# Activations of 32 tokens by gathered rows, U products of 352 columns, 20 odd chunks and 24 gathers in the gate stage

## The chip, the cores and the metric

The kernel runs on one core of a Trainium2 chip. The metric is the device time of one execution in microseconds (us). The kernel before took 1524.5 us, the median of 3 runs (1523.61 to 1525.55).

## What is computed

One decoder block for 512 tokens of width 1024, all in float32: attention and gated linear attention side by side, then a mixer over 16384 experts (PEER), then a final norm. The change lies in the mixer. Each token picks 128 experts (8 heads with 16 each) by two rounds of top-16 and gets a gate for each; every expert has a row of `u` and a row of `v`.

```python
def peer_ffn(h, wq, subkeys, u, v):
    ...
    expert = jnp.take_along_axis(cand_i, best_pos, axis=-1)
    gates = jax.nn.softmax(best_v, axis=-1).astype(h.dtype)
    ...
    def block(args):
        xb, eb, gb = args
        ub = jnp.take(u, eb, axis=0)
        hid = jax.nn.gelu(jnp.einsum('tkd,td->tk', ub, xb), approximate=False) * gb
        vb = jnp.take(v, eb, axis=0)
        return jnp.einsum('tk,tkd->td', hid, vb)
```

## The kernel before

The 512 tokens are four blocks of 128. Blocks 0 to 2 are the dense ones (`DENSE`, 384 tokens, `TD`): for them PE multiplies with all 16384 experts, in 128 chunks of 128 experts, and the gates, written out as a dense matrix that is zero for experts that were not picked, select. Block 3 (`GB`, the gathered block) gets its rows of `u` and `v` by 128 + 128 gathers, each of 128 rows of 4 KB (one expert for each token), and DVE multiplies and adds them up.

A float32 product is made of three products in the fp32r form (`mm3`, L68 to L71): each operand is split into a high part (a copy by ACT, L64) and a low part (a subtraction by DVE or POOL, L65).

**U part** (`u_part`, L692). For a chunk c, PE makes 8 x 3 = 24 products of a 128x128 piece of `u` by the tokens' activations; the result `ph` has one column for each dense token but the last `TS` = 16 (`TU` = 368 columns). ACT takes the Gelu (L705) into `ge`. The chunks of `AHEAD`, the 64 even ones, are computed ahead, while queries, routing and gates are made; their `ge` goes to DRAM (`gsp`, on ACT's queue) and is read back later. The 64 odd ones are computed in the V stage, each some 8 chunks ahead of its use (`LEAD`), and stay in a ring of `RING` = 6.

**Sparse rows** (`sp_index`, `sp_rows`, `sp_gather`, `sp_dot`, `sp_finish`, L930 to L975). The last 16 dense tokens get their activations otherwise: each gather fetches 128 rows of `u` (16 tokens by 8 of their 128 experts), and DVE makes the dot products with the tokens' own rows, 16 gathers and 16 dots in all, with 2 buffers. The result times the gate replaces the gate of these tokens, so that the dense gate matrix already holds the activation there.

**Gate stage.** For each dense block and each group of 16 tokens, `gate_group` makes one-hot matrices on DVE (`o12`, L895), multiplies them by the gates (`o2`, L911), and PE multiplies the two (`pg`, 24 short products each half group, L918); ACT copies the result (L920), and it is stored as `Gd` in DRAM. There are 24 groups, each with two halves. In this stage the order of DVE and POOL is that of the program (`manual_schedule`); PE, ACT and SP are ordered by the scheduler. A loop over the pieces of work (`woven`, `work`) keeps a running sum of what DVE and PE were given, by written costs (`DVE_ALL`, `PE_ALL`, `UCOST`), and calls the next U chunk whenever PE's share falls behind. The pieces are the groups, the sparse dots between their halves, the routing of the blocks, and at the end of the stage `EARLY` = 8 of the gathered block's 128 dots (`ahead`, `dots_of`), one after each group of the third block. One-hot matrices and gathered rows share a ring of 5 buffers (`gr`, `GR`).

**V stage.** For each of the 128 chunks, `v_part` loads the rows of `v` (two chunks a load), splits them, multiplies the gates by the Gelu values (L1169), splits the product (`Ah` L1173, `Al` L1174, four buffers each), and PE adds 18 products of 512 columns into the six accumulators (`v_matmuls`). After every second chunk comes the next odd U chunk. `gather_to` spreads the remaining gathers over the chunks: `gather_u` (a gather of `u` rows on POOL, a dot on DVE, L1003) and `gather_v` (a gather of `v` rows, added into `gacc`, L1016), with 7 buffers. At the end `finish` scales each block, adds the residual, norms it and stores it; the gathered block is finished after the last gather, then the dense blocks with the last four chunks (`LAST`).

## Time and profile before

| what | before |
|---|---|
| median of 3 runs | 1524.5 us |
| the profiled execution: its time | 1523.26 us |
| the profiled execution: its span | 1521.5 us |
| granted TensorE clock, mean | 0.991 |
| PE busy | 1460.3 us (96%) |
| DVE busy | 1251.6 us (82%) |
| ACT busy | 677.7 us (45%) |
| POOL busy | 482.2 us (32%) |
| moved by DMA | 417.04 MB, mean 274 GB/s |
| PE's share of the chain that ended last | 89% |

The stages follow one another: conditioning, projections and both mixers to about 290 us, queries and top-k to about 420, routing and gates to about 705, the V stage to about 1503, the last norms to the end. Busy times are per engine; matmuls overlap in their rows, so the distance from start to start is their cost.

### The profile page before, as it was taken

How to read it: one execution, taken by the hardware profiler on the slowest of the kernel's cores; microseconds unless marked ns; L12 is line 12 of the kernel's file. 1: busy time of each engine (PE TensorE's matmuls, PEld its weight loads, DVE VectorE, ACT ScalarE, POOL GpSimd, SP SyncE). 2: the span in 40 equal slices, each digit the busy share in tenths (PEclk: the TensorE clock that was granted, in tenths of full speed). 3: DMA queues.
4: the chain of work that ended last, by engine and by line, in shares of the span. 5: the costliest groups of instructions: out<-in, count | busy, mean ns of one | idle time of the engine just before them, and what ended most of it. 6: DMA issues, size and time to landing. Idle time of an engine off the chain costs nothing.

```text
span 1521.5 us, 24401 instructions
## 1 busy us (share of the span) xinstructions
PE 1460.3 (96%) x9387; PEld 1301.7 (86%) x9387; DVE 1251.6 (82%) x2389; ACT 677.7 (45%) x1072; POOL 482.2 (32%) x344
## 2 busy tenths in 40 slices
PE   4999989899999999999999999999999999999995
PEld 3787877888999999999888888888888888888884
DVE  7578657689999999996778878787878878788998
ACT  5545486533344665765333333333333333333332
POOL 1000000145505220222334434453535434454461
PEclk9999999999999999999999999999999999999997
DMA  9253535462446997899999989989999898998894
GB/s 349 99 208 115 175 106 191 152 215 92 140 171 207 305 314 229 257 295 330 411 408 335 334 317 345 357 322 333 343 349 344 326 339 344 357 335 291 312 356 157
DMA packets 158004, 417.04 MB, mean 274 GB/s; under 512 B 11312, under 2 KB 78144, under 8 KB 145472
## 3 DMA queue, kind: packets, MB, share of 16 engines
q1 hardware_dynamic: 107296, 258.18, 47.5%
q0 software_dynamic: 39312, 144.20, 25.9%
q10 hardware_dynamic: 11280, 13.11, 2.5%
q8 instruction: 73, 1.20, 0.3%
q14 instruction: 43, 0.35, 0.1%
HBM read 374.01 MB, written 41.42 MB: 273 GB/s over the span
## 4 chain that ended last, share of the span: by engine, by line
PE 89%; DVE 4%; ACT 3%; DMA 2%; issue 2%; SPq 0%; DVEq 0%; POOL 0%; ACTq 0%; POOLq 0%
PE ph L71 11%; PE ph L69 11%; PE acc L70 11%; PE acc L69 11%; PE ph L70 11%; PE acc L71 11%; PE pg L918 4%; PE pq L69 2%; PE pq L71 2%; PE pq L70 2%; PE pj L71 1%; PE pj L69 1%; PE pj L70 1%; DMA gu<-in_u_dram,ix_u 1%; PE pn L69 1%
## 5 line engine op out<-in xcount | busy, mean ns | idle before, releaser
L993 POOL DMA_INDIRECT gu<-in_u_dram,ix_u x128 | 191.4, 1495 | 314.4 <-DVE gacc L1016 128.8
L1011 POOL DMA_INDIRECT gv<-in_vP_dram,ix_v x128 | 176.8, 1381 | 216.2 <-DVE gu L1003 163.9
L1173 ACT ACTIVATE Ah<-gr 128x384 fp32r<-128x384 f32 x128 | 67.1, 525 | 308.6 <-PE acc L70 305.0
L1016 DVE SCALAR_TENSOR_TENSOR gacc<-gv,hg,gacc 128x1024 f32<-128x1024 f32 x127 | 162.8, 1282 | 0.2
L1003 DVE SCALAR_TENSOR_TENSOR gu<-gu,h2n 128x1024 f32<-128x1024 f32 x128 | 156.0, 1220 | 0.7 <-DMA gu<-in_u_dram,ix_u 0.7
L705 ACT ACTIVATE ge<-ph 128x368 f32<-128x368 f32 x128 | 59.9, 468 | 152.8 <-PE ph L71 152.7
L1174 DVE TENSOR_TENSOR Al<-gr,Ah 128x384 fp32r<-128x384 f32 x128 | 71.0, 556 | 66.4 <-ACT Ah L1173 66.2
L920 ACT ACTIVATE gs<-pg 128x512 f32<-128x512 f32 x96 | 94.1, 1114 | 3.8 <-PE pg L918 2.8
L1066 POOL IOTA iot<- 128x256 bf16 x1 | 1.5, 1540 | 282.2 <-DVE h2Tl L680 282.2
L911 DVE TENSOR_TENSOR o<-o,gp 128x3072 bf16<-128x3072 bf16 x48 | 84.0, 1755 | 0.4 <-PE pg L918 0.4
L959 POOL DMA_INDIRECT spr<-in_u_dram,spix x16 | 40.6, 2535 | 105.6 <-DVE spr L964 61.3
L918 PE MATMUL pg<-o,o 128*128 128x128 bf16 x1152 | 72.7, 218 | 0.5 <-ACT gs L920 0.5
L918 PEld LDWEIGHTS <-o 128*128 128x128 bf16 x1152 | 66.2, 97 | 6.0 <-issue 0.7
L895 DVE TENSOR_TENSOR o<-iot,t 128x2048 bf16<-128x2048 bf16 x48 | 58.4, 1223 | 2.4 <-PE pg L918 2.4
L1169 DVE TENSOR_TENSOR gr<-ge,gr 128x368 f32<-128x368 f32 x64 | 34.5, 540 | 23.3 <-ACT ge L705 23.3
L217 DVE SCALAR_TENSOR_TENSOR macc<-wa,scs,macc 128x1024 f32<-128x1024 f32 x28 | 38.8, 1385 | 5.1 <-DMA wa<-in_w_ada_dram 4.8
L1169 DVE TENSOR_TENSOR gr<-gel,gr 128x368 f32<-128x368 f32 x64 | 31.9, 535 | 2.9 <-DMA gr<-Gd 2.9
L70 PE MATMUL pq<-h2Tl,wq_0h 128*128 128x512 f32 (+1 forms) x80 | 27.9, 349 | 1.2 <-DVE h2Tl L680 1.2
L69 PE MATMUL pq<-h2Th,wq_0h 128*128 128x512 f32 (+1 forms) x80 | 28.0, 352 | 1.0 <-ACT qha L758 1.0
L71 PE MATMUL pq<-h2Th,wq_1l 128*128 128x512 f32 (+1 forms) x80 | 28.1, 352 | 0.0
L70 PE MATMUL pq<-h2Tl,wq_1h 128*128 128x512 f32 (+1 forms) x80 | 28.1, 352 | 0.0
L69 PE MATMUL pq<-h2Th,wq_1h 128*128 128x512 f32 (+1 forms) x80 | 28.0, 350 | 0.0
(2608 smaller groups left out, 5028.3 us busy)
## 6 DMA issues: line engine op xcount, KB each, us to landing
u<-in_uT_dram SPq DMA_DIRECT2D x64, 1024.0 KB, 8.3
v<-in_vP_dram SPq DMA_DIRECT2D x64, 1024.0 KB, 7.5
Gd<-gs SPq DMA_DIRECT2D x23, 1024.0 KB, 8.1
gr<-Gd SPq DMA_DIRECT2D x15, 1536.0 KB, 11.0
wa<-in_w_ada_dram SPq DMA_DIRECT2D x20, 1024.0 KB, 6.3
gsp<-ge ACTq DMA_DIRECT2D x64, 184.0 KB, 4.6
gel<-gsp SPq DMA_DIRECT2D x32, 368.0 KB, 4.8
wi<-in_w_in_dram SPq DMA_DIRECT2D x9, 1024.0 KB, 6.2
```

What stands on the lines that cost most here:

```text
L69: nc.tensor.matmul(acc, lh, rh, start=start, stop=False)
L70: nc.tensor.matmul(acc, lh, rl, start=False, stop=False)
L71: return nc.tensor.matmul(acc, ll, rh, start=False, stop=stop)
L911: nc.vector.tensor_tensor(o2, o12[:, :, 1, None].to_broadcast([P, H, 3, P, 2]), gp3[:, g0:g0 + H, :, None].to_broadcast([P, H, 3, P, 2]), ...
L918: nc.tensor.matmul(pt[:, i, :], o12[:, g, 0, :, r], o2[:, g, m, :, r], start=(m == 0), stop=(m == 2))
L920: nc.scalar.activation(gs[:, :, t0 + 4 * f:t0 + 4 * f + 4].rearrange("p b a -> p a b"), pt, AF.Copy)
L993: nc.gpsimd.indirect_dma_start(out=ur, out_offset=None, in_=a["u"], in_offset=bass.IndirectOffsetOnAxis(ap=ix_u[:, s:s + 1], axis=0))
L1003: nc.vector.scalar_tensor_tensor(ur, ur, 1.0, h2n, op0=OP.mult, op1=OP.mult, accum_out=hid[:, s:s + 1])
L1011: nc.gpsimd.indirect_dma_start(out=vr, out_offset=None, in_=a["vP"], in_offset=bass.IndirectOffsetOnAxis(ap=ix_v[:, s:s + 1], axis=0))
L1016: nc.vector.scalar_tensor_tensor(gacc, vr, hg[:, s:s + 1], gacc, op0=OP.mult, op1=OP.add)
L1173: nc.scalar.activation(grp(Ah), A, AF.Copy)
L1174: nc.vector.tensor_tensor(grp(Al), A, grp(Ah), OP.subtract)
```

## The change

- `TS` goes from 16 to 32 tokens: 32 sparse gathers and dots instead of 16, each of 32 tokens by 4 experts, with 3 buffers and up to three dots a group; the U products have 352 columns instead of 368.
- `AHEAD` gets 20 odd chunks beside the 64 even ones: chunks 4m+1 and 4m+3 for m = 2, 5, ..., 29. The V stage makes 44 U chunks instead of 64. `gsp` is laid out anew so that two odd chunks are read back at once, into a buffer of their own (`gel1`, one; `gel0`, two).
- `EARLY` goes from 8 to 24: two gathers after each group from the middle of the second block on, and their two dots one group later.
- The remaining gathers are spread by a written cost of each chunk instead of evenly, without the lag of 10 between `u` and `v` rows, over the first 118 chunks (`LAST_G`), and the gathered block is finished when chunk 119 is reached.

```diff
--- before.py
+++ after.py
@@ -30,14 +30,15 @@
 GB = 3
 TG = 16
 NGRP = TD // TG
-TS = 16
+TS = 32
 TU = TD - TS
 NGU = TU // TG
 SB = DENSE[-1]
 SR = P // TS
 
 
-AHEAD = tuple(range(0, P, 2))
+ODD_AHEAD = tuple(range(2, 32, 3))
+AHEAD = tuple(c for m in range(P // 4) for c in (4 * m, 4 * m + 2) + ((4 * m + 1, 4 * m + 3) if m in ODD_AHEAD else ()))
 RING = 6
 GR = 5
 TCARGS = dict(schedule_with_timeline_sim=True)
@@ -686,7 +687,7 @@
                     nc.tensor.transpose(pb[:, i * P:(i + 1) * P], h32[:, 4 * half + i, :], ident)
                 nc.scalar.activation(h2n[:, half * 512:(half + 1) * 512], pb, AF.Copy)
 
-    gsp = dr.tile([len(AHEAD), P, TU], F32, name="gsp")
+    gsp = dr.tile([P // 4, 2, 2, P, TU], F32, name="gsp")
     ges, last_gelu = {}, {}
 
     def u_part(c, lo_eng=None, after=None):
@@ -703,8 +704,8 @@
         ge = dnA.tile([P, NGU, TG], F32, tag="ge", bufs=RING, name=f"ge{c}")
         gef = ge.rearrange("p g t -> p (g t)")
         last_gelu["u"] = nc.scalar.activation(gef, ph, AF.Gelu)
-        if c % 2 == 0:
-            nc.scalar.dma_start(gsp[c // 2], gef)
+        if c in AHEAD:
+            nc.scalar.dma_start(gsp[c // 4, c % 2, c // 2 % 2], gef)
         else:
             ges[c] = ge
         return end
@@ -950,20 +951,20 @@
             ps_, cs = slice(r * TS, (r + 1) * TS), slice(r * TS, (r + 1) * TS)
             nc.sync.dma_start(sp["ix"][ps_], e[P - TS:, cs])
             nc.sync.dma_start(sp["g"][ps_], gates[SB][P - TS:, cs])
-        for j in range(2):
+        for j in range(3):
             sp_gather(j)
         yield 0.3, 0
 
     def sp_gather(j):
-        sp[j] = rt.tile([P, D], F32, tag="spr", bufs=2, name=f"spr{j}")
+        sp[j] = rt.tile([P, D], F32, tag="spr", bufs=3, name=f"spr{j}")
         nc.gpsimd.indirect_dma_start(out=sp[j], out_offset=None, in_=a["u"],
                                      in_offset=bass.IndirectOffsetOnAxis(ap=sp["ix"][:, j:j + 1], axis=0))
 
     def sp_dot(j):
         r = sp.pop(j)
         nc.vector.scalar_tensor_tensor(r, r, 1.0, sp["x"], op0=OP.mult, op1=OP.mult, accum_out=sp["hid"][:, j:j + 1])
-        if j + 2 < TS:
-            sp_gather(j + 2)
+        if j + 3 < TS:
+            sp_gather(j + 3)
         yield 1.15, 0
 
     def sp_finish():
@@ -986,7 +987,7 @@
 
     gather_tile.k = -1
 
-    EARLY = 8
+    EARLY = 24
 
     def fetch_u(s):
         ur = gather_tile(f"gu{s}") if s >= EARLY else gp.tile([P, D], F32, tag="gr", bufs=GR, name=f"gu{s}")
@@ -1016,9 +1017,9 @@
             nc.vector.scalar_tensor_tensor(gacc, vr, hg[:, s:s + 1], gacc, op0=OP.mult, op1=OP.add)
 
 
-    VLAG = 10
-    gathers = [(s * 0.88 / NS, gather_u, s) for s in range(NS)]
-    gathers += [((s + VLAG) / (NS + VLAG), gather_v, s) for s in range(NS)]
+    gathers = [(-1, gather_u, s) for s in range(EARLY)]
+    gathers += [((s - EARLY) * 0.88 / (NS - EARLY), gather_u, s) for s in range(EARLY, NS)]
+    gathers += [((s + 0.5) / NS, gather_v, s) for s in range(NS)]
     gathers = [g[1:] for g in sorted(gathers, key=lambda g: g[0])]
 
     def gather_to(upto):
@@ -1093,7 +1094,7 @@
         for q in range(P // TG):
             for i, piece in enumerate(gate_group(DENSE.index(n), n, q)):
                 yield piece
-                if (i == 3 or i == 1 and q % 2 == 0) and rows:
+                if i and rows:
                     yield from sp_dot(rows.pop(0))
             if q in extra:
                 yield from chain(*extra[q])
@@ -1103,14 +1104,19 @@
     first_block = {3: [gate_transposes(1)], 5: [gate_parts(1)], 6: [gate_rest(1)]}
     second_block = {1: [route(GB)], 2: [gathered_index()], 3: [sp_finish()], 5: [gate_transposes(SB)],
                     6: [gate_parts(SB)], 7: [gate_rest(SB)]}
-    third_block = {0: [ahead(0, 1)]}
-    for q in range(1, EARLY):
-        third_block[q] = [dots_of(q - 1, 1), ahead(q, 1)]
-    third_block[EARLY - 1] += [dots_of(EARLY - 1, 1)]
+    third_block = {}
+    places = [(second_block, q) for q in range(3, 8)] + [(third_block, q) for q in range(P // TG)]
+    for i, (block, q) in enumerate(places):
+        pieces = block.setdefault(q, [])
+        if i:
+            pieces.append(dots_of(2 * i - 2, 2))
+        if i < EARLY // 2:
+            pieces.append(ahead(2 * i, 2))
+    assert EARLY == 2 * len(places) - 2
     work = chain(route_heads(), *head, woven(0, rows, first_block), woven(1, rows, second_block),
                  woven(SB, [], third_block))
     NL_U = len(AHEAD) - LAST_U
-    DVE_ALL = 11 + 4 * 7.6 + 3 + 1.15 * TS + 2.82 * 2 * NGRP + 9 + 1.14 * (NL_U - WQ_U)
+    DVE_ALL = 11 + 4 * 7.6 + 3 + 1.15 * TS + 2.82 * 2 * NGRP + 1.15 * EARLY + 1.14 * (NL_U - WQ_U)
     PE_ALL = 1.4 * 2 * NGRP + 3 + UCOST * (NL_U - WQ_U)
     dve_s = ExitStack()
     dve_s.enter_context(tc.manual_schedule(engines={mybir.EngineType.DVE, mybir.EngineType.Pool}))
@@ -1158,11 +1164,11 @@
         if c % CG == 2 and c + CG < P:
             gates_of(c // CG + 1)
         vh, vl = hilo(v_part.raw[:, c % 2], [P, D], f"vc{c}", nc.vector)
-        if c % 2 == 0:
-            if c % 4 == 0:
-                v_part.ge = dnA.tile([P, 2, TU], F32, tag="gel", bufs=2, name=f"gel{c}")
-                nc.sync.dma_start(v_part.ge, gsp[c // 2:c // 2 + 2].rearrange("c p t -> p c t"))
-            ge = v_part.ge[:, c // 2 % 2].rearrange("p (g t) -> p g t", g=NGU)
+        if c in AHEAD:
+            if c % 4 < 2:
+                v_part.ge[c % 2] = dn.tile([P, 2, TU], F32, tag=f"gel{c % 2}", bufs=2 - c % 2, name=f"gel{c}")
+                nc.sync.dma_start(v_part.ge[c % 2], gsp[c // 4, c % 2].rearrange("c p t -> p c t"))
+            ge = v_part.ge[c % 2][:, c // 2 % 2].rearrange("p (g t) -> p g t", g=NGU)
         else:
             ge = ges.pop(c)
         A = v_part.g[:, :, c % CG, :]
@@ -1173,6 +1179,8 @@
         nc.scalar.activation(grp(Ah), A, AF.Copy)
         nc.vector.tensor_tensor(grp(Al), A, grp(Ah), OP.subtract)
         return c, Ah, Al, vh, vl
+
+    v_part.ge = {}
 
     def v_matmuls(parts, blocks=range(len(DENSE)), qs=(0, 1)):
         for c, Ah, Al, vh, vl in parts:
@@ -1203,16 +1211,21 @@
                 nc.vector.scalar_tensor_tensor(y[:, qs], y[:, qs], r, fwb[:, qs], op0=OP.mult, op1=OP.mult)
             nc.sync.dma_start(out[n * P:(n + 1) * P, qs], y[:, qs])
 
-    LEAD = 8
+    LEAD, LAST_G = 8, 118
+    cost = [4.09 + (UCOST if c % 2 == 0 and c + 1 + LEAD < P and c + 1 + LEAD not in AHEAD else 0) for c in range(LAST_G)]
     for c in range(1, 1 + LEAD, 2):
         u_part(c)
     for c in range(P - LAST):
-        if c % 2 == 0 and c + 1 + LEAD < P:
+        if c % 2 == 0 and c + 1 + LEAD < P and c + 1 + LEAD not in AHEAD:
             u_part(c + 1 + LEAD)
         with tc.issue_after(last_gelu["u"].ins) if c < 2 else nullcontext():
             parts = v_part(c)
         v_matmuls([parts])
-        gather_to(len(gathers) * (c + 1) // (P - LAST))
+        gather_to(EARLY + int((len(gathers) - EARLY) * sum(cost[:c + 1]) / sum(cost) + 1e-6))
+        if c == LAST_G + 1:
+            with tc.issue_after(last_gelu["u"].ins), tc.issue_after(last_gelu["hg"].ins):
+                nc.scalar.preload_act_table_set("natural_log_exp_and_others")
+            finish(GB, [gacc[:, 0:512], gacc[:, 512:1024]])
         if c == 16:
             tc.keep_in_program_order(bcast_load(fwb, a["fw"], D))
         if c == P - 16:
@@ -1225,9 +1238,6 @@
                 for i in range(4):
                     nc.tensor.matmul(pb[:, i * P:(i + 1) * P], ones, dg[:, 4 * q + i, :], start=True, stop=True)
                 nc.scalar.activation(h2n[:, q * 512:(q + 1) * 512], pb, AF.Copy)
-    with tc.issue_after(last_gelu["u"].ins), tc.issue_after(last_gelu["hg"].ins):
-        nc.scalar.preload_act_table_set("natural_log_exp_and_others")
-    finish(GB, [gacc[:, 0:512], gacc[:, 512:1024]])
     last = [v_part(c) for c in range(P - LAST, P)]
     xl = dn.tile([P, 2, D], F32, tag="vraw", bufs=2, name="xl")
     for i in range(len(DENSE)):
```

DVE in the first block of the gate stage, some half groups in (`o` from `iot` is a one-hot, `o` from `gp` its product with the gates, `spr` a sparse dot, `uc..l` the low part of a U chunk). Before:

```order
L964 SCALAR_TENSOR_TENSOR spr_4902,sphid<-spr_4902,xs 128x1024
L895 TENSOR_TENSOR o_012_5273<-iot,t_5034 128x2048
L65 TENSOR_TENSOR uc52l<-u_5275,uc52h 128x1024
L911 TENSOR_TENSOR o_010_5309<-o_08_5204,gp_5043 128x3072
L895 TENSOR_TENSOR o_016_5339<-iot,t_5034 128x2048
L911 TENSOR_TENSOR o_018_5341<-o_012_5273,gp_5043 128x3072
L964 SCALAR_TENSOR_TENSOR spr_5202,sphid<-spr_5202,xs 128x1024
L65 TENSOR_TENSOR uc54l<-u_5275,uc54h 128x1024
L895 TENSOR_TENSOR o_020_5408<-iot,t_5034 128x2048
L911 TENSOR_TENSOR o_020_5410<-o_016_5339,gp_5043 128x3072
L964 SCALAR_TENSOR_TENSOR spr_5269,sphid<-spr_5269,xs 128x1024
```

and now:

```order
L965 SCALAR_TENSOR_TENSOR spr_5228,sphid<-spr_5228,xs 128x1024
L896 TENSOR_TENSOR o_016_5405<-iot,t_5062 128x2048
L66 TENSOR_TENSOR uc46l<-u_5338,uc46h 128x1024
L965 SCALAR_TENSOR_TENSOR spr_5267,sphid<-spr_5267,xs 128x1024
L912 TENSOR_TENSOR o_018_5442<-o_012_5336,gp_5071 128x3072
L965 SCALAR_TENSOR_TENSOR spr_5332,sphid<-spr_5332,xs 128x1024
L66 TENSOR_TENSOR uc45l<-u_5475,uc45h 128x1024
L896 TENSOR_TENSOR o_020_5511<-iot,t_5062 128x2048
L912 TENSOR_TENSOR o_020_5513<-o_016_5405,gp_5071 128x3072
L965 SCALAR_TENSOR_TENSOR spr_5403,sphid<-spr_5403,xs 128x1024
L66 TENSOR_TENSOR uc47l<-u_5475,uc47h 128x1024
```

Of eleven rows three were sparse dots and two U chunks; now four are sparse dots and three U chunks, two of them odd (45, 47). The order of one-hot and product is kept, with more between them.

DVE in the V stage, from chunk 12 on (`vc..l` low part of the rows of `v`, `Al` low part of the gated activations, `gu` a dot of a gathered row, `gacc` an addition of one). Before:

```order
L65 TENSOR_TENSOR vc12l<-v_8936,vc12h 128x1024
L65 TENSOR_TENSOR vc13l<-v_8936,vc13h 128x1024
L65 TENSOR_TENSOR uc23l<-u_8903,uc23h 128x1024
L1169 TENSOR_TENSOR gr_8833<-ge_8934,gr_8833 128x23x16
L1016 SCALAR_TENSOR_TENSOR gacc<-gv_9105,hg,gacc 128x1024
L1003 SCALAR_TENSOR_TENSOR gu_9172,hid<-gu_9172,h2n 128x1024
L1174 TENSOR_TENSOR Al_9151<-gr_8833,Ah_9150 128x384
L65 TENSOR_TENSOR vc14l<-v_9037,vc14h 128x1024
L65 TENSOR_TENSOR vc15l<-v_9037,vc15h 128x1024
L1174 TENSOR_TENSOR Al_9185<-gr_8833,Ah_9184 128x384
L1016 SCALAR_TENSOR_TENSOR gacc<-gv_9175,hg,gacc 128x1024
L65 TENSOR_TENSOR uc25l<-u_9108,uc25h 128x1024
```

and now:

```order
L1008 TENSOR_TENSOR hg<-hg,gg_g 128x8
L1180 TENSOR_TENSOR Al_9718<-gr_9132,Ah_9717 128x384
L66 TENSOR_TENSOR vc12l<-v_9610,vc12h 128x1024
L1017 SCALAR_TENSOR_TENSOR gacc<-gv_9506,hg,gacc 128x1024
L66 TENSOR_TENSOR vc13l<-v_9610,vc13h 128x1024
L1004 SCALAR_TENSOR_TENSOR gu_9571,hid<-gu_9571,h2n 128x1024
L1017 SCALAR_TENSOR_TENSOR gacc<-gv_9574,hg,gacc 128x1024
L1180 TENSOR_TENSOR Al_9785<-gr_9542,Ah_9784 128x384
L1004 SCALAR_TENSOR_TENSOR gu_9577,hid<-gu_9577,h2n 128x1024
L66 TENSOR_TENSOR vc14l<-v_9677,vc14h 128x1024
L66 TENSOR_TENSOR vc15l<-v_9677,vc15h 128x1024
L66 TENSOR_TENSOR uc25l<-u_9742,uc25h 128x1024
```

Before, a U chunk's low part stands behind every pair of chunks of `v` (23, 25); now 23 is gone from this place, since it was made ahead, and more dots and additions of gathered rows stand between the pairs.

DVE at the end (`y` from `gacc` is the gathered block's scaling, `y` from `acc` a dense block's). Before:

```order
L65 TENSOR_TENSOR vc126l<-v_14636,vc126h 128x1024
L1016 SCALAR_TENSOR_TENSOR gacc<-gv_14546,hg,gacc 128x1024
L65 TENSOR_TENSOR vc127l<-v_14636,vc127h 128x1024
L1016 SCALAR_TENSOR_TENSOR gacc<-gv_14549,hg,gacc 128x1024
L1016 SCALAR_TENSOR_TENSOR gacc<-gv_14579,hg,gacc 128x1024
L1016 SCALAR_TENSOR_TENSOR gacc<-gv_14582,hg,gacc 128x1024
L1016 SCALAR_TENSOR_TENSOR gacc<-gv_14585,hg,gacc 128x1024
L1192 TENSOR_TENSOR y_14589<-gacc,h2n 128x512 x2
L1192 TENSOR_TENSOR y_14681<-acc_8177,h2n 128x512
L1192 TENSOR_TENSOR y_14681<-acc_8178,h2n 128x512
L1192 TENSOR_TENSOR y_14730<-acc_8179,h2n 128x512
L1192 TENSOR_TENSOR y_14730<-acc_8180,h2n 128x512
```

and now:

```order
L1017 SCALAR_TENSOR_TENSOR gacc<-gv_14457,hg,gacc 128x1024
L1017 SCALAR_TENSOR_TENSOR gacc<-gv_14460,hg,gacc 128x1024
L1180 TENSOR_TENSOR Al_14729<-gr_14287,Ah_14728 128x384
L1200 TENSOR_TENSOR y_14551<-gacc,h2n 128x512 x2
L1201 TENSOR_TENSOR y_14551<-y_14551,xf_14552 128x512
L66 TENSOR_TENSOR vc126l<-v_14712,vc126h 128x1024
L1201 TENSOR_TENSOR y_14551<-y_14551,xf_14552 128x512
L66 TENSOR_TENSOR vc127l<-v_14712,vc127h 128x1024
L1203 TENSOR_TENSOR ssf_14554<-ssf_14554 128x1
L81 TENSOR_SCALAR rf3m<-ssf_14554 128x1
L84 TENSOR_TENSOR rf3t<-rf3y 128x1
L85 TENSOR_TENSOR rf3t<-rf3t,rf3m 128x1
```

Four additions into `gacc` and the gathered block's scaling stood behind the last low part (`vc127l`), with the dense blocks' work right behind; now the additions end ahead of `vc126l`, and that block's output is on its way before a dense block's begins.

## The prediction

> **What bounds the kernel now.** I read the stretches first: busy time of every engine over one stretch each. Columns: stretch, its length, PE, weight load, DVE, ACT and POOL busy with instruction counts, granted clock, DMA share, GB/s.
>
> ```profile
> 405.00:440.00 35.00, 35.00 (x212) 35.00 (x211) 32.54 (x174) 16.14 (x21) 10.28 (x12) 1.00 0.51 179
> 440.00:480.00 40.00, 40.00 (x246) 39.85 (x245) 37.46 (x56) 16.01 (x27) 16.65 (x2) 1.00 0.55 192
> 480.00:510.00 30.00, 30.00 (x261) 29.29 (x260) 28.10 (x27) 16.88 (x22) 8.40 (x5) 1.00 0.78 255
> 510.00:540.00 30.00, 30.00 (x290) 29.15 (x287) 30.00 (x29) 20.01 (x28) 6.92 (x4) 1.00 1.00 315
> 540.00:600.00 60.00, 60.00 (x502) 58.86 (x500) 57.32 (x64) 34.73 (x44) 8.60 (x5) 1.00 0.87 286
> 600.00:660.00 60.00, 59.22 (x604) 57.32 (x603) 55.30 (x47) 43.47 (x54) 11.78 (x3) 1.00 0.81 250
> 660.00:705.00 45.00, 45.00 (x438) 43.87 (x437) 40.83 (x38) 29.65 (x36) 8.58 (x5) 1.00 0.99 315
> 705.00:740.00 35.00, 32.04 (x185) 30.67 (x182) 17.98 (x25) 13.49 (x22) 9.93 (x10) 0.96 0.96 362
> 740.00:800.00 60.00, 60.00 (x296) 52.87 (x295) 49.78 (x68) 21.82 (x32) 24.75 (x18) 1.00 1.02 405
> 800.00:1100.00 300.00, 300.00 (x1472) 263.93 (x1471) 245.27 (x321) 108.43 (x153) 133.23 (x94) 1.00 0.91 337
> 1100.00:1400.00 300.00, 300.00 (x1479) 264.57 (x1478) 243.33 (x318) 108.98 (x154) 130.01 (x93) 1.00 0.92 340
> ```
>
> PE is busy without a hole from 405 to 600 and from 740 to 1400, with some 4 us missing between. In the gate stage (about 420 to 705) DVE is nearly as full, 281.5 of 300 us from 405 to 705; in the V stage it has 18% left. A busy PE need not be at its peak, so I checked the pace in the order of time (start, length, instruction).
>
> ```profile
> 409.22 0.33 PE L69 MATMUL ph<-h2Th,uc12h 128*128 128x368 f32 x1
> 413.22 0.33 PE L69 MATMUL ph<-h2Th,uc14h 128*128 128x368 f32 x1
> ...
> 1498.14 0.39 PE L69 MATMUL acc<-vc127h,Ah 128*128 128x512 f32 x1
> ...
> 1502.22 0.39 PE L69 MATMUL acc<-vc127h,Ah 128*128 128x512 f32 x1
> ```
>
> The first two are the starts of neighbouring U chunks of 24 products: 4.00 us, 166.7 ns each, back to back. Between the other two stand 18 products of 512 columns: 4.08 us, 226.7 ns. From the two widths a column costs 0.417 ns and each product 13 ns beside. So PE streams at one column rate all the time, and only less matmul work, or its few holes, can shorten the run. The waits name the holes (engine, line, cause: us, times, longest).
>
> ```profile
> PE acc L69 <- ACT Ah L1173: 1.9, 1, 1.9
> ...
> PE acc L69 <- ACT vc118h L64: 1.3, 1, 1.3
> ...
> PE ph L71 <- DVE uc124l L65: 1.0, 1, 1.0
> ```
>
> Nothing longer stands after 290 us until the last product.
>
> **Narrower U products.** All 128 chunks keep 24 products and go from 368 to 352 columns: 16 columns by 0.417 ns is 6.67 ns each, 0.16 us a chunk (4.00 to 3.84), 128 x 0.16 = **20.5 us** of PE work. All of it lies in stretches without holes, so I count all of it, as long as nobody else becomes late. Below zero this cannot go: no product is added.
>
> **Twenty odd chunks go ahead.** PE work is only moved: 20 x 3.84 = 76.8 us leave the V stage and enter the gate stage. With them go 20 subtractions on DVE, 20 stores on ACT's queue, and their read-back in the V stage.
>
> **Sixteen more sparse rows, sixteen more early gathers.** This is DVE work in the gate stage, 32 dots. Groups by line, and rows in the order of time:
>
> ```profile
> L1003 DVE SCALAR_TENSOR_TENSOR gu<-gu,h2n 128x1024 f32<-128x1024 f32 x128 | 156.0, 1220 | 0.7 <-DMA gu<-in_u_dram,ix_u 0.7
> L911 DVE TENSOR_TENSOR o<-o,gp 128x3072 bf16<-128x3072 bf16 x48 | 84.0, 1755 | 0.4 <-PE pg L918 0.4
> L895 DVE TENSOR_TENSOR o<-iot,t 128x2048 bf16<-128x2048 bf16 x48 | 58.4, 1223 | 2.4 <-PE pg L918 2.4
> ...
> L964 DVE SCALAR_TENSOR_TENSOR spr<-spr,xs 128x1024 f32<-128x1024 f32 x16 | 19.5, 1222 | 4.6 <-DMA spr<-in_u_dram,spix 4.6
> ```
>
> ```profile
> 706.75 1.22 DVE L65 TENSOR_TENSOR uc126l<-u,uc126h 128x1024 fp32r<-128x1024 f32 x1
> 707.89 1.22 DVE L65 TENSOR_TENSOR uc1l<-u,uc1h 128x1024 fp32r<-128x1024 f32 x1
> ```
>
> A row of 1.22 us is followed by the next start after 1.14 us, so I take 0.08 us off each length. DVE gains 32 x 1.14 + 20 x 1.14 = 59 us in the gate stage, PE gains 76.8 and loses about 70 chunks x 0.16 = 11, net 66. Whether PE stays the longer one is read per token group of 16. The chain gives the gate products:
>
> ```profile
> 497.64 2.77 PE pg L918 x48
> ```
>
> In the first block the changed order puts 20 U chunks and 24 sparse dots into 8 groups. DVE: two one-hots and two products 2 x (1.14 + 1.67) = 5.62, three dots 3.42, 2.5 subtractions 2.85, together 11.9 us; PE: 2.77 + 2.5 x 3.84 = 12.4. In the last block, with 16 U chunks and two early dots a group: DVE 5.62 + 2.28 + 2.28 = 10.2, PE 2.77 + 2 x 3.84 = 10.5. So PE stays the longer one, by 3 to 4%, about 10 us over 24 groups, which is what DVE may lose in new waits before PE pays. The waits of DVE that are there already:
>
> ```profile
> DVE spr L964 <- DMA spr<-in_u_dram,spix: 4.6, 2, 2.7
> DVE hg L1007 <- ACT hg L1006: 3.3, 1, 3.3
> ...
> DVE o L895 <- PE pg L918: 2.4, 4, 0.8
> ```
>
> A sparse row is asked for when the dot three before it is done, one group (12.4 us) earlier; less the dot itself, 11.2 us remain. Issue to landing is 8.4 us in the middle (transfer table):
>
> ```profile
> gu<-in_u_dram,ix_u POOLq DMA_INDIRECT x128, 8.2
> ...
> spr<-in_u_dram,spix POOLq DMA_INDIRECT x16, 8.4
> ```
>
> Behind a late dot stand the next one-hot, the next U subtraction and with it PE. I expect several short waits, mostly inside the 10 us, and charge PE 2 us (bounds 0 and 20). The early gathers wait a group too and hold 2 of the 5 buffers of the one-hots; three one-hots still fit, so I charge nothing, with up to 0.8 us for each of 13 groups (the L895 row) as the other end. The 20 stores on ACT's queue take 0.33 us of issue each,
>
> ```profile
> 698.24 0.33 ACTq L707 DMA_DIRECT2D gsp<-ge  x1
> ```
>
> 7 us in a stage where ACT is under 75% busy in every stretch above: nothing, and if ACT had no room, at most those 7 us.
>
> **The V stage.** Per V chunk DVE pays now 245.27 / 50 = 4.91 us of 6.0 (300 us hold 50 chunks). Its gathers are counted by the transfer table of 800 to 1400, which holds 100 chunks:
>
> ```profile
> gu<-in_u_dram,ix_u POOLq DMA_INDIRECT x95, 8.1
> gv<-in_vP_dram,ix_v POOLq DMA_INDIRECT x91, 7.9
> ```
>
> From 1.86 a chunk they rise to 232 / 118 = 1.97, and U chunks fall from 0.5 to 40 / 118 = 0.34: 4.91 - 0.16 x 1.14 + 0.11 x 1.2 = 4.86 us in 4.08 + 0.34 x 3.84 = 5.38 us, 90% instead of 82%. In runs of four to six V chunks with no U chunk between them it is higher still; four buffers of weights level that out. DVE's largest wait there is for ACT, whose buffers PE holds:
>
> ```profile
> DVE Al L1174 <- ACT Ah L1173: 65.6, 59, 3.6
> ```
>
> So DVE runs ahead of PE, and this slack goes first. I charge 2 us (bounds 0 and 15). Where the stages meet, one U chunk fewer covers the way of the last gates through DRAM:
>
> ```profile
> 702.53 2.93 PE L918 MATMUL pg<-o,o 128*128 128x128 bf16 x48
> ```
>
> ```profile
> 723.61 0.54 DVE L1169 TENSOR_TENSOR gr<-gel,gr 128x368 f32<-128x368 f32 x1 [2.93 <-DMA gr<-Gd]
> ```
>
> The gates were back 18 us after the last gate product; 6 x 3.84 = 23 us of U products stand there then, where 28 stood, so the cover holds by 5 us, and without it the rest of the way would be PE's.
>
> **The end.** The sequence block's gathers end with chunk 117 and its output is finished by chunk 119, not behind the last gather.
>
> ```profile
> 1502.67 0.39 PE L71 MATMUL acc<-vc127h,Al 128*128 128x512 f32 x1
> ...
> 1491.53 5.25 DVE L1016 SCALAR_TENSOR_TENSOR gacc<-gv,hg,gacc 128x1024 f32<-128x1024 f32 x4
> ...
> 1504.10 1.28 DVE L1192 TENSOR_TENSOR y<-acc,h2n 128x512 f32<-128x512 f32 x2
> ...
> 1512.74 3.43 DVE L1203 SCALAR_TENSOR_TENSOR y<-y,rf2y,fwb 128x512 f32<-128x512 f32 x2
> ```
>
> From the last product (1503.1) to the last scaling 9.7 us pass, because DVE still has the gathered block's tail between. Without that block it is a product, an addition and a square (0.64 each), one other block's scaling (1.4) and small steps (2): about 5 us. I take **5 us** off (bounds 2 and 6).
>
> **Sum**, against the profiled execution (span 1521.5, its time 1523.3): 1523.3 - 20.5 - 5 + 2 + 2 = 1501.8. The median of the runs shown lies 1.2 us above that execution: **1503 us**.
>
> **Rivals.**
> *Transfers bind the V stage.* Mean 338 GB/s at a share of 0.915 there; per V chunk 6.0 us x 338 = 2.03 MB. The change trades U loads (0.16 x 0.52 = 0.08 MB less) for denser gathers (0.11 x 0.52 = 0.06 more) and read-backs (0.03 more), so 2.03 MB must pass in 5.38 us: 377 GB/s. For it: 338 / 0.915 = 369 GB/s would be full. Against it: 405 ran from 740 to 800 with PE whole. At 369 each chunk takes 5.50 us, 118 x 0.12 = 14 us: 1517.
> *The same ceiling, lower: slower than before.* From the rate R on where 118 x (2.03 / R - 5.38) exceeds 21.5 us, R below 365 GB/s, the move of U work buys nothing; at 358 GB/s it is 34 us, 1537. The Trainium skill, "DMA: Bandwidth & Descriptors", section "Where 436 GB/s comes from", has the HBM side bind HBM transfers at about 358 GB/s, and notes that its measured rates are with the neighbouring core idle; the 405 of this trace disagrees, so the chance is small.
> *Sparse rows come late.* If the doubled density lifts landing from 8.4 to 12 us, 29 dots wait about 0.8 us: 23 us less the 5 spare in those groups, 1521.
> *The narrower product is not faster.* Then only the end counts: 1523. The equal pace law of both widths speaks against it.
>
> **How the numbers follow.** Forecast 0.72 (its own range 1496 to 1510); transfers at 369 GB/s 0.11; below 365 GB/s 0.05; sparse rows late 0.09, half of it short of 1521; no faster product 0.03. The range 1496 to 1518 leaves out the last three and the worst of the second. 0.2% is 3 us, about what can be told: faster 0.90, same 0.04, slower 0.06.
>
> **What would show it.** U chunks 3.84 us apart; PE busy in full across a gate stage longer by 66 us and a V stage shorter by about 87; the sparse dots' wait on their transfer under 10 us in sum; the transfer rate near 377 GB/s in the V stage; the last scaling about 5 us after the last product. PE holes in the V stage behind v loads or the hi parts would prove me wrong, as would DVE waits of over 10 us on rows in the gate stage.

## The result and the profile after

The changed kernel takes 1533.8 us (median of 7 runs, 1529.1 to 1540.7) where the kernel before takes 1524.5 us (7 runs, 1523.6 to 1527.1): ratio 1.0057, 95% interval 1.0036 to 1.0077. It is slower by about half a per cent; 1503 us, faster, was forecast. The profiled execution is one of 1533.85 us (span 1532.1 us, granted clock 0.986).

Busy time by stage, cut at the last top-k product, the end of the last gate product, the first product of V0 and the last V product. Columns: stretch, its length, PE, weight load, DVE, ACT and POOL busy with instruction counts, granted clock, DMA share, GB/s. The kernel before:

```profile
403.10:708.00 304.90, 303.08 (x2563) 296.88 (x2562) 285.78 (x443) 179.81 (x232) 72.53 (x39) 1.00 0.79 255
708.00:736.40 28.40, 26.50 (x159) 26.19 (x158) 11.91 (x17) 7.57 (x13) 9.03 (x9) 1.00 1.00 379
736.40:1502.90 766.50, 765.15 (x3736) 671.42 (x3736) 637.54 (x827) 278.01 (x395) 339.36 (x240) 1.00 0.91 338
1502.90:1521.50 18.60, 0.16 (x1) 0.00 (x0) 12.44 (x37) 5.81 (x22) 2.93 (x2) 0.56 0.31 113
```

The changed kernel:

```profile
409.60:784.00 374.40, 372.46 (x3047) 365.66 (x3046) 346.49 (x530) 207.70 (x274) 127.66 (x71) 1.00 0.86 288
784.00:811.30 27.30, 20.85 (x131) 20.55 (x129) 5.09 (x7) 6.18 (x11) 7.19 (x8) 0.93 0.96 362
811.30:1515.20 703.90, 684.20 (x3280) 587.89 (x3280) 600.90 (x793) 251.80 (x362) 294.42 (x225) 1.00 0.92 348
1515.20:1532.10 16.90, 0.20 (x1) 0.00 (x0) 7.99 (x26) 4.28 (x14) 3.25 (x2) 0.57 0.25 94
```

The gate stage is 69.5 us longer (66 were forecast) and PE is whole in it. The V stage is 62.6 us shorter. Of the 87 us that were forecast for the U work, 82 lie here (19 chunks of 4.00 us fewer, and 0.16 us on each of the other 40); the rest is one U chunk in the stretch ahead of it. So 20 us are missing: 703.90 us with PE busy for 684.20, where before 766.50 held 765.15. The stretch between the stages is 1.1 us shorter, the end 1.7 us. These sum to 4 us more; the other 6.5 us between the two profiled executions lie ahead of 409.6 us, 5.8 of them ahead of the first query product, up to which no engine's order differs (see e8).

The waits of PE in the changed kernel from 780 us on (engine, line, cause: us, times, longest):

```profile
PE acc L70 <- ACT Ah L1179: 6.5, 1, 6.5
PE acc L70 <- ACT vc28h L65: 1.6, 1, 1.6
PE acc L70 <- ACT vc40h L65: 1.5, 1, 1.5
PE acc L70 <- ACT vc52h L65: 1.5, 1, 1.5
...
PE acc L70 <- ACT vc12h L65: 1.4, 1, 1.4
...
PE acc L70 <- ACT vc24h L65: 1.3, 1, 1.3
PE acc L70 <- ACT vc60h L65: 1.3, 1, 1.3
...
PE acc L71 <- DVE vc116l L66: 1.0, 1, 1.0
```

Before, one wait for a high part stood in the whole V stage (vc118h, 1.3 us). Now there are twelve, most of them twelve chunks apart (V28, V40, V52 to V100; V12, V24, V60), the period of the odd chunks that went ahead. Here is ScalarE in the order of time, around V28 (start, length, instruction, idle time before it and what ended it):

```profile
953.27 0.53 ACT L1179 ACTIVATE Ah<-gr 128x384 fp32r<-128x384 f32 x1 [0.71 <-PE acc L71]
957.35 0.53 ACT L1179 ACTIVATE Ah<-gr 128x384 fp32r<-128x384 f32 x1 [3.55 <-PE acc L71]
961.77 0.53 ACT L1179 ACTIVATE Ah<-gr 128x384 fp32r<-128x384 f32 x1 [3.89 <-PE acc L71]
965.52 0.46 ACT L706 ACTIVATE ge<-ph 128x352 f32<-128x352 f32 x1 [3.22 <-PE ph L72]
965.88 0.20 ACT L1007 ACTIVATE hg<-hid 128x8 f32<-128x8 f32 x1
965.98 1.05 ACT L65 ACTIVATE vc28h<-v 128x1024 fp32r<-128x1024 f32 x1
```

and PE beside it:

```profile
965.16 0.32 PE L72 MATMUL ph<-h2Th,uc37l 128*128 128x352 f32 x1
967.08 1.65 PE L70 MATMUL acc<-vc28h,Ah 128*128 128x512 f32 x6 [1.59 <-ACT vc28h L65]
```

ScalarE is idle for 11 of these 13 us. It stands in its fixed order at three roundings of gate products (`Ah`), each waiting for one of four buffers that a V chunk on PE frees, and then at the Gelu of U37, which waits for the U chunk that PE is doing. Only behind it comes the high part of V28, which PE wants at once. So Gelu, `hg` and rounding (0.46, 0.20, 1.05 us, overlapping) stand on PE's path.

### The profile page after: what moved, and what is told of

It is laid out like the page before. It is cut to its first block, busy times and chain, and to the rows that moved or that the text cites. A ratio compares the mean times of both kernels' runs of the same rounds, so it can differ in the third digit from the quotient of the medians.

```text
span 1532.1 us, 24455 instructions
## 1 busy us (share of the span) xinstructions
PE 1449.0 (95%) x9387; PEld 1285.5 (84%) x9387; DVE 1264.8 (83%) x2421; ACT 676.4 (44%) x1072; POOL 490.8 (32%) x360
## 5 line engine op out<-in xcount | busy, mean ns | idle before, releaser
L994 POOL DMA_INDIRECT gu<-in_u_dram,ix_u x128 | 183.2, 1431 | 304.5 <-DVE gacc L1017 112.4
L1012 POOL DMA_INDIRECT gv<-in_vP_dram,ix_v x128 | 161.3, 1260 | 204.5 <-DVE gu L1004 110.6
L960 POOL DMA_INDIRECT spr<-in_u_dram,spix x32 | 72.4, 2264 | 105.8 <-DVE spr L965 69.2
L706 ACT ACTIVATE ge<-ph 128x352 f32<-128x352 f32 x128 | 57.9, 452 | 106.6 <-PE ph L72 106.5
L1175 DVE TENSOR_TENSOR gr<-gel,gr 128x352 f32<-128x352 f32 x84 | 39.5, 519 | 17.7 <-DMA gr<-Gd 17.7
L965 DVE SCALAR_TENSOR_TENSOR spr<-spr,xs 128x1024 f32<-128x1024 f32 x32 | 39.0, 1220 | 3.1 <-DMA spr<-in_u_dram,spix 3.1
```

The lines of the kernel that those rows point to most:

```text
L960: nc.gpsimd.indirect_dma_start(out=sp[j], out_offset=None, in_=a["u"], in_offset=bass.IndirectOffsetOnAxis(ap=sp["ix"][:, j:j + 1], axis=0))
L994: nc.gpsimd.indirect_dma_start(out=ur, out_offset=None, in_=a["u"], in_offset=bass.IndirectOffsetOnAxis(ap=ix_u[:, s:s + 1], axis=0))
L1012: nc.gpsimd.indirect_dma_start(out=vr, out_offset=None, in_=a["vP"], in_offset=bass.IndirectOffsetOnAxis(ap=ix_v[:, s:s + 1], axis=0))
```

## The experiments

**e1: the high part first in ScalarE's order.** `hi_of["last"]` is the high part of V chunk c, `issue_after` fixes an order on one engine without a wait, and `gelu()` is the Gelu's line with its store, taken out of `u_part`.

```diff
-        last_gelu["u"] = nc.scalar.activation(gef, ph, AF.Gelu)
...
-        nc.scalar.activation(grp(Ah), A, AF.Copy)
+        with tc.issue_after(hi_of["last"].ins) if c >= 2 else nullcontext():
+            nc.scalar.activation(grp(Ah), A, AF.Copy)
...
+        if gelu and c >= 2:
+            with tc.issue_after(hi_of["last"].ins):
+                gelu()
```

> The changed kernel with one thing more: in ScalarE's fixed order the Gelu of U chunk c+9 and the rounding of gate product c (Ah) stand behind the high part of V chunk c, not ahead of it. Theory A (order): the dozen holes of 1.3 to 1.6 us on TensorE at V12, V24, V28, V40, ... are there because the high part of the next V pair stands in ScalarE's order behind an instruction that waits for the U or V chunk that TensorE is just doing (Ah behind 'acc', ge behind 'ph'); the V pair's load landed long before. Then nearly all 12 go, first to last V product falls from 703.7 us to 685-690, total 1514 to 1520 us. Theory B (transfers): the V pairs land too late because the transfers stand at 93 to 97 % in the V stage; then the holes stay and the time is 1530 to 1537. Theory C (clock): what is lost ahead of the gate stage (5.8 us up to the first query product) is a dip of the granted clock, not the change; then the first query product starts between 271 and 277 us here too, whatever the rest does.

Measured: 1505.3 us (1504.9 to 1506.7), 0.9877 of before, interval 0.9862 to 0.9892. The same stages:

```profile
403.50:777.50 374.00, 372.32 (x3046) 365.50 (x3045) 346.14 (x530) 207.85 (x274) 127.13 (x71) 1.00 0.86 289
777.50:806.50 29.00, 22.80 (x132) 22.22 (x130) 5.18 (x7) 6.13 (x11) 7.19 (x8) 0.94 0.93 343
806.50:1489.00 682.50, 679.64 (x3280) 587.51 (x3280) 599.45 (x800) 250.39 (x370) 307.63 (x225) 1.00 0.95 359
1489.00:1503.20 14.20, 0.21 (x1) 0.00 (x0) 6.93 (x18) 2.65 (x9) 2.48 (x2) 0.68 0.30 111
```

ScalarE and PE at V28:

```profile
953.48 1.04 ACT L67 ACTIVATE vc28h<-v 128x1024 fp32r<-128x1024 f32 x1
954.43 0.51 ACT L1187 ACTIVATE Ah<-gr 128x384 fp32r<-128x384 f32 x1
957.36 0.47 ACT L709 ACTIVATE ge<-ph 128x352 f32<-128x352 f32 x1 [2.42 <-PE ph L74]
```

```profile
957.00 0.32 PE L74 MATMUL ph<-h2Th,uc37l 128*128 128x352 f32 x1
957.16 1.54 PE L72 MATMUL acc<-vc28h,Ah 128*128 128x512 f32 x6
```

The high part is ready 2.6 us before its first product, and V28 follows U37 without a hole. The V stage falls by 21.4 us to 682.5, near the 684 us of the forecast (766.5 less 82). Theory A holds, with more gained than the 1514 to 1520 us that were expected. Theory B falls: the transfers run faster than in the changed kernel while PE is whole, as this stretch of e1 shows,

```profile
1100.00:1150.00 50.00, 50.00 (x243) 43.26 (x242) 43.27 (x58) 15.88 (x23) 25.15 (x21) 1.00 1.00 394
```

so the 348 GB/s of the changed kernel's V stage were no ceiling. e1 is also faster than both kernels, by 1.2% against before. One reserve: the scheduler lays out the V stage anew, and in e1 and e11 the order on VectorE, SyncE and PE changed there too (behind the first six products of V28, PE now does six of the low part in a row, where it alternated between two kinds). In e5, the next experiment, the other engines kept theirs but for a handful of instructions.

**e5 and e11: the two halves of that edit.** e5 has the Gelu's lines of the diff alone, e11 those of `Ah` alone.

> Half of the edit of e1: only the Gelu of U chunk c+9 stands behind the high part of V chunk c; the Ah roundings keep their place. In ScalarE's order of this kernel Ah still stands ahead of the high parts of V12, V24, V36, V60. Theory: each of the two kinds of instruction makes the holes of its own place: those at the start of a run with U chunks (V28, V40, V52, ...) go or shrink where the Gelu was last, those at V12, V24, V60 stay; 6 to 9 of 12 holes gone, total 1512 to 1524 us. Rival: Ah alone is the cause (it waits for the V chunk that has just been done, whatever the Gelu does): nearly all holes stay, 1527 to 1535. Rival: the Gelu alone: as e1, 1503 to 1508.

> The other half of e1's edit: only Ah of chunk c stands behind the high part of V chunk c; the Gelu keeps its place. In ScalarE's order the Gelu of U37 and of U109 still stand right ahead of the high parts of V28 and V100, while at V12, V24, V60 the Gelu ahead is that of a U chunk done long before, and at V40 and V116 no Gelu stands there. Theory: holes stay where the U chunk of that Gelu is the one TensorE does just then (V28, V100 and their like, 2 to 5 of 12), the rest goes; with e5 (7.7 us of holes gone of 19.7) the halves add up to about e1: total 1507 to 1515 us. Rival (both halves are needed for any one hole, or one alone does it all): 1525 or more, or 1503 to 1506.

Measured: e5 1520.9 us (0.9972, interval 0.9958 to 0.9986), e11 1519.8 us (0.9963, 0.9950 to 0.9976). In e5 the waits at V40, V52, V64 and V88 are gone, at V76 and V100 0.9 us for the low part are left, V28 shrinks to 1.1, and those at V12, V24, V60 stay at 1.3 to 1.4, as expected. e11 missed its expectation of 1507 to 1515: no wait for a high part is left, but a new one for `Ah`, which now stands behind Gelu and high part:

```profile
PE acc L72 <- ACT Ah L1182: 14.2, 7, 3.6
```

One of the seven, of 3.6 us, lies ahead of V0. The other six are at V28, V40, V52, V64, V76 and V100 (1.0 to 2.7 us), just where e5 took the Gelu out of the way; those that e5 kept (V12, V24, V60) are gone here.

Idle time of PE from the first to the last V product, added up over the gaps between products, is 19.7 us in the changed kernel, 12.0 in e5, 12.6 in e11, 2.8 in e1. Each half takes 7 to 8 us and both 17: it is not one instruction that stands wrong, but whichever one waits for PE's current work ahead of PE's next operand.

**e10: the same 20 odd chunks, at another place.**

```diff
-ODD_AHEAD = tuple(range(2, 32, 3))
+ODD_AHEAD = tuple(range(22, 32))
```

> The changed kernel with the same count of odd chunks ahead, 20, but the last ones (from 89 on) in place of pairs spread over all: one U chunk per two V chunks up to V79, from there V chunks alone; ScalarE's order is left to the scheduler. In its order three Ah roundings stand ahead of the high part of every fourth V chunk from V92 on, and none in that place before V79. Theory A (order; it needs a stretch of V chunks without U products, whatever the transfers do): no holes for a high part up to V78, and 7 to 10 holes of 1.3 to 1.5 us at every fourth V chunk from V84 or so on; V stage 695 to 703 us, total 1522 to 1534. Rival (the holes come where the pattern changes, or from the transfers of the U pairs that stand side by side): one or two holes in all, total 1505 to 1518.

Measured: 1527.9 us (1.0024, interval 1.0013 to 1.0035). The longest of PE's waits from 830 us on:

```profile
PE acc L70 <- ACT vc108h L65: 3.4, 1, 3.4
PE acc L71 <- DVE vc100l L66: 1.5, 1, 1.5
PE acc L70 <- ACT vc100h L65: 1.4, 1, 1.4
PE acc L70 <- ACT vc92h L65: 1.4, 1, 1.4
PE acc L70 <- ACT vc112h L65: 1.4, 1, 1.4
PE acc L70 <- ACT vc88h L65: 1.3, 1, 1.3
PE acc L70 <- ACT vc104h L65: 1.3, 1, 1.3
PE acc L70 <- ACT vc116h L65: 1.3, 1, 1.3
PE acc L70 <- ACT vc96h L65: 1.3, 1, 1.3
...
```

The holes moved with the odd chunks: none before V88, then one at every fourth V chunk. Idle time within the V stage is 17.6 us in sum, 2.4 of them at V0. So a stretch of V chunks without U products makes the holes. At V12, V24 and V60 of the changed kernel, as in e10, no U chunk of 3.84 us stands right ahead that would hide the late high part. At V28, V40, V52 to V100 one does, the first U chunk after such a stretch, and the high part stands behind its Gelu.

**e6: the order edit on the kernel before, as a control.** The diff is e1's, on the other kernel.

> The kernel before with e1's edit of ScalarE's order and nothing else (a control). Theory: before the change the regular pattern has no such holes (no wait of TensorE for a high part above 0.1 us in its V stage), so the edit is worth nothing there: 1522 to 1527 us. Rival: the edit helps any V stage, and e1's gain says nothing of the change: 1500 to 1515.

Measured: 1523.4 us, 0.9989 (0.9978 to 0.9999). In the regular pattern of one U chunk for two V chunks there was nothing to mend; e1's gain belongs to the change.

**e2 and e4: parts of the change.** e2 is the kernel before with the 32 tokens alone (first three pairs of lines; `gel` also moves to another buffer pool, as in the change), e4 the changed kernel without odd chunks (last pair):

```diff
-TS = 16
+TS = 32
...
-        sp[j] = rt.tile([P, D], F32, tag="spr", bufs=2, name=f"spr{j}")
+        sp[j] = rt.tile([P, D], F32, tag="spr", bufs=3, name=f"spr{j}")
...
-                if (i == 3 or i == 1 and q % 2 == 0) and rows:
+                if i and rows:
...
-ODD_AHEAD = tuple(range(2, 32, 3))
+ODD_AHEAD = ()
```

> The kernel before with 32 gathered tokens alone (U products of 352 columns, three row buffers, up to three row products a gate group; the pair tile of early activations moved to another pool): even chunks ahead and 8 gathers of the sparse block as before. It tells the narrower product from the moved chunks. Theory A: the regular pattern of one U chunk per two V chunks stays, so no holes of 1.5 us come up in the V stage; U products 160 ns, 64 chunks x 0.16 = 10 us less in the V stage (766 to about 756 us); VectorE takes 16 row products x 1.15 = 18 us more in the gate stage, of which TensorE's longer share hides some: 302 us becomes 296 to 308. Total 1508 to 1520 us. Rival (a narrower product is no gain where the transfers bind): V stage stays at 764 to 767, total 1522 to 1530.

> The changed kernel without the 20 odd chunks ahead (even chunks only); 32 gathered tokens, 24 early gathers and the new spread of the gathers stay. Theory A (the irregular pattern of U chunks makes the holes): the V stage has one U chunk per two V chunks again and no holes of 1.5 us, 754 to 758 us from first to last V product; VectorE binds the gate stage (37 us of row and gather products more than before, 10 us less of U products on TensorE): 315 to 330 us. Total 1520 to 1535 us. Rival B (the new spread of gathers or the transfers make the holes): PE holes of 15 to 20 us in the V stage here too, total 1540 or more.

Measured: e2 1551.4 us (1.0161, interval 1.0136 to 1.0186), e4 1573.5 us (1.0315, 1.0292 to 1.0338). Both are far above what was expected. Gate and V stage of e2, then of e4:

```profile
408.40:729.60 321.20, 303.22 (x2556) 292.19 (x2554) 302.43 (x474) 179.17 (x232) 97.17 (x55) 0.98 0.81 265
...
760.40:1525.00 764.60, 755.32 (x3736) 661.68 (x3736) 633.11 (x822) 275.38 (x391) 340.68 (x240) 0.99 0.91 338
```

```profile
404.80:765.00 360.20, 313.27 (x2556) 298.91 (x2554) 321.82 (x508) 179.08 (x234) 119.26 (x71) 0.95 0.79 260
...
795.60:1560.00 764.40, 755.04 (x3736) 662.35 (x3736) 625.32 (x814) 280.93 (x409) 315.89 (x224) 0.99 0.88 328
```

PE's work in the V stage is the expected 755 us, 10 less than before: the narrower product pays. The 9 us of idle time beside it lie at the stage's two ends, behind the low part of V0 (5.5 and 8.0 us) and the high parts of V118 and V119; between them PE is whole, which also clears the new spread of the gathers. But the gate stage opens by 16 and 55 us. In e4 PE idles 47 us there, 34 of them before U products that wait for a Gelu on ScalarE:

```profile
PE ph L70 <- ACT ge L706: 34.0, 11, 6.7
```

DVE is not full either (321.8 of 360.2 us). ScalarE's order shows why those Gelus come late. In the eight longest of these waits (1.3 us and more, 31.4 us together) the Gelu stands right behind the high part of a later U chunk, and in five of them (23.7 us) that one waits for its load. Here are ScalarE and PE in e4:

```profile
719.58 1.06 ACT L65 ACTIVATE uc120h<-u 128x1024 fp32r<-128x1024 f32 x1 [8.02 <-DMA u<-in_uT_dram]
720.55 0.45 ACT L706 ACTIVATE ge<-ph 128x352 f32<-128x352 f32 x1
```

```profile
721.04 0.66 PE L70 MATMUL ph<-h2Th,uc116h 128*128 128x352 f32 x1 [5.80 <-ACT ge L706]
```

So it is again an order on ScalarE, with the roles turned; why the load is late stays open. What matters for the change: its 20 odd chunks bring 77 us of products and lengthen the gate stage by only 14 us (360.2 to 374.4), and with them PE is whole. Without them the other parts lose, in the order that the scheduler gives them. Whether another order or earlier loads would close e4's holes too was not measured, so the 16 and 55 us are not the price of the added dots alone.

**e3, e7 and e9: the hole ahead of V0.** The last gates go to DRAM and come back. Before, their write and GpSimd's read of the first chunk group were issued 6.4 us apart:

```profile
707.34 0.38 ACTq L923 DMA_DIRECT2D Gd<-gs  x1
...
713.75 0.58 POOL L1146 DMA_DIRECT2D gr<-Gd  x1 [17.43 <-DMA Gd<-gs]
```

In the changed kernel they are 14.7 us apart:

```profile
783.58 0.38 ACTq L924 DMA_DIRECT2D Gd<-gs  x1
...
798.27 0.58 POOL L1152 DMA_DIRECT2D gr<-Gd  x1 [26.64 <-DMA gsp<-ge]
```

e3 leaves four early U chunks for this stretch; e7 is e1 with write and read on SyncE's queue and the next V and U loads behind the read; e9 also splits the read so that gathers should stand behind it.

```diff
-    WQ_U, LAST_U, LEAD_U, UCOST = 11, 2, 4.0, 24 * (TU / 2400 + 0.0133)
+    WQ_U, LAST_U, LEAD_U, UCOST = 11, 4, 4.0, 24 * (TU / 2400 + 0.0133)
```

```diff
-        queue = nc.scalar if bi * (P // TG) + q == NGRP - 1 else nc.sync
-        queue.dma_start(Gd[:, :, bi * (P // TG) + q].rearrange("c p e -> p c e"),
+        gate_group.write = nc.sync.dma_start(Gd[:, :, bi * (P // TG) + q].rearrange("c p e -> p c e"),
...
-            nc.sync.dma_start(v_part.raw, vPc[c:c + 2].rearrange("c i d -> i c d"))
+            with tc.issue_after((gates_of.first if c else gate_group.write).ins) if c < 4 else nullcontext():
+                nc.sync.dma_start(v_part.raw, vPc[c:c + 2].rearrange("c i d -> i c d"))
```

```diff
+            tc.keep_in_program_order(nc.gpsimd.dma_start(to[:, :h], Gd[j][:, :h]))
+            gates_of.first = nc.sync.dma_start(to[:, h:], Gd[j][:, h:])
```

> The changed kernel with four early U chunks, not two, left for the stretch between the gate stage and the first V chunk (LAST_U 4). Theory: the 6.5 us hole ahead of V0 is the gates' way through DRAM, 24 us from the last gate product, with 23 us of U products of which some run early; two chunks more (7.7 us) fill it: hole 0 to 1 us, the gate stage 7 us shorter, total 6 us less than the changed kernel (1526 to 1530). Rival: the gates' way is longer because more loads go ahead of it when the stage ends, and two chunks more bring their loads along; then the hole stays at 4 us or more, time 1531 to 1537.

> The kernel of e1, and the last block of gates is written and read back by SyncE's queue with the second V pair and the next U pair behind the read; of before, the read came 6 us after the write, in e1 it came 15.6 us after, with 3.4 MB of V, U and early-activation loads issued within 3 us of the write. Theory: those loads share the transfer engines with the last gates and make the way of the gates 9 us longer, which leaves 3.6 + 2.6 + 1.1 us of holes on TensorE; then the read is issued 5 to 8 us after the write, the hole ahead of V0 goes, and the total is 1498 to 1502 us. Rival: the way of the gates is set by something else (ScalarE's and VectorE's work on V0), or the loads that are held back make a hole at V2 of 3 us or more: 1504 to 1509.

> The kernel of e7, and the read of the last gates is split in halves, one on SyncE's and one on GpSimd's queue, so that the gathers too stand behind it. In e7 the V and U loads were held back, but GpSimd was free and issued a gather every 1.3 to 3 us instead; the read came 15.3 us after the write. Theory: the way of the gates is as long as what else the transfer engines are given in it; with only the first V pair beside it (1 MB) the read is issued 5 to 9 us after the write, the hole ahead of V0 goes from 6.7 us to under 2 us, and the total is 1498 to 1503 us if nothing is late behind it. Rival 1: the read comes sooner, but gathers, V2 or U pairs are late behind it and give the time back: 1503 to 1508. Rival 2: the way stays at 13 us or more: transfers were not its reason.

Measured: e3 1538.7 us (1.0104, interval 1.0085 to 1.0123), e7 1506.2 (0.9869, 0.9851 to 0.9887), e9 1512.5 (0.9928, 0.9912 to 0.9944). None gained against the kernel it was made from (e3 the changed kernel, e7 and e9 e1), and e3 and e9 lie above their rivals' ranges as well. In e3 the stretch still has 7 us of holes, and its V stage has more holes for high parts than the changed kernel's. In e7 the loads left were replaced by gathers from a GpSimd queue that no longer stood behind the read, and the read came 15.3 us after the write. In e9 it came 9.6 us after, but its first half did not depend on the last gates and did not hold the gathers, and an 8.7 us wait of U products for a Gelu came up instead. That the transfers beside it lengthen the way of the gates is therefore likely, not shown, and what a shorter way is worth stays open.

**e8: the changed kernel again.**

> The changed kernel once more, on the chip of e5 to e7. Up to the first query product nothing differs between the kernels in any engine's order, and that point lay between 270.5 and 276.6 us in six traces. Theory C (chance of the granted clock and of transfers): it comes at another time than 276.85 us here, 270.5 to 276, and the median is 1529 to 1535. Rival (the change itself lengthens the front): 276 to 278 us again.

Measured: 1530.0 us (1.0032, interval 1.0017 to 1.0047), first query product at 274.2 us, V stage 704.2 us. In thirteen traces that product came between 269.8 and 276.9 us with one and the same order ahead of it (271.1 before, 270.7 in e1, 276.9 in the changed kernel's first trace). So the 6 us there vary from execution to execution and do not come from a changed order; what the change costs is the 4 us of the later stages, near the 4.5 us between the medians of this run (1530.0 and 1525.5); the first seven runs gave 9.3.

## Why the prediction was wrong

- **Narrower products, 3.84 us a chunk:** right. U products stand 0.16 us apart, and e2 and e4 show the 10 us in the V stage by themselves.
- **Gate stage, PE stays the longer engine, +66 us:** right, +69.5. Sparse rows were not late, as this wait of DVE in the changed kernel's gate stage shows (3.1 us in 4 times); e4, 55 us longer than before in this stage, shows how much hung on the odd chunks.

```profile
DVE spr L965 <- DMA spr<-in_u_dram,spix: 3.1, 4, 1.1
```

- **Transfers bind (two rivals):** wrong in both versions; e1 moved 394 GB/s over 50 us with PE whole. The Trainium skill, "DMA: Bandwidth & Descriptors", section "Where 436 GB/s comes from", has HBM transfers bound at about 358 GB/s; the 394 GB/s of this trace, with one core at work, lie above that.
- **V stage, "four buffers of weights level that out", 2 us (bounds 0 and 15):** this step failed. Measured: 19.7 us of idle time and PE busy 4.6 us longer than in e1 for the same 3280 recorded products. I weighed DVE's share, 82 to 90%, and DVE was not the one. ScalarE, busy a third of the time, was: the buffers are only of use if the instruction that fills the next one is not queued behind one that waits for PE. The prediction did name the sign, "PE holes in the V stage behind v loads or the hi parts", but gave it no price and no rival.
- **Between the stages, "the cover holds by 5 us":** wrong. The read was issued 14.7 us after the write, not 6.4, and 6.5 us of hole ate what one U chunk less was to save (1.1 in place of 4 or 5).
- **The end, 5 us:** mis-sized. It is 1.7 us shorter in the changed kernel. The last scaling starts 6.0 us after the last product instead of 9.7, near the 5 of the forecast, but from there to the end of the span 10.7 us pass instead of 8.8:

```profile
1521.37 2.42 DVE L1211 SCALAR_TENSOR_TENSOR y<-y,rf2y,fwb 128x512 f32<-128x512 f32 x2
```

In e1 the end is 4.4 us shorter than before (18.6 to 14.2). That is not the work of the mended order: e4, without that edit, ends in 13.9 us as well.

From the forecast's 1501.8 us for the profiled execution to the 1533.85 us measured, 32 us are missing: about 18 in the V stage, 4 between the stages, 3 at the end, 1 to 2 in the gate stage, and 6.5 ahead of it, which the forecast could not know. With the order in the V stage mended the total comes out, 1505.3 us measured in e1 against 1503, but partly by luck: in e1 the stretch between the stages is 0.6 us longer where the forecast had it 5 shorter, and the V stage 84.0 us shorter where, with the 2 us charged, it had 80.

## What to carry to other kernels

Work that is taken out of a steady loop is also a cover: ask which late instruction its time was hiding, and look at the engine that prepares the next operand, however idle it is. In an in-order engine an instruction that waits for what TensorE is doing now must not stand ahead of the one that TensorE needs next; where a scheduler sets the order, read it at the places where the pattern changes, and pin it. A busy share says nothing of that.

## What the hardware showed beside

A hole costs more than its length. The first six products of V28 take 1.54 us without a hole (e1), 1.65 after one of 1.59 us (the changed kernel, granted clock 1.00 over the 3 us from there on), and 2.15 after one of 2.00 us in e11, where the clock fell to half:

```profile
960.33 2.15 PE L72 MATMUL acc<-vc28h,Ah 128*128 128x512 f32 x6 [2.00 <-ACT Ah L1182]
```

The stretch behind that hole, in the columns of the stages (granted clock 0.51):

```profile
961.20:964.20 3.00, 3.00 (x9) 2.32 (x8) 3.00 (x4) 2.75 (x5) 0.00 (x0) 0.51 0.07 27
```

The length of the hole does not decide that by itself in these runs: behind 1.91 us at V76 in e11 and 3.4 us at V108 in e10 the clock stayed at 1.00. Where holes are many the granted clock is lower too: 0.95 over e4's gate stage with 47 us of idle PE, 1.00 over the changed kernel's with 2.
